# Two chained transformer blocks on one core: in the paired FFN products, high parts a piece ahead of low parts, two of four block sums on GpSimd, and later transposes

## The chip, the cores and the metric

The kernel runs on one core of a Trainium2 chip. The metric is the device time of one execution in microseconds. Five engines take part: TensorE (PE in the profile; its weight loads are PEld), VectorE (DVE), ScalarE (ACT), GpSimd (POOL) and SyncE (SP), which here only issues DMAs. Each engine works through its own instructions in order and waits for the others by semaphores.

## The reference

Two blocks work on 256 tokens of width 2048, in float32. The first holds three attention branches, the second a gated recurrence, a convolution and the FFN in which the change lies:

```python
x = x + jnp.einsum('bse,ed->bsd', mixed, w_out[l])
h2 = _rmsnorm(x, ffn_norm_w[l])
g, u = jnp.split(jnp.einsum('bsd,df->bsf', h2, w_gate_up[l]), 2, axis=-1)
x = x + jnp.einsum('bsf,fd->bsd', jax.nn.silu(g) * u, w_down[l])
```

`w_gate_up` is 2048 x 11264 and `w_down` 5632 x 2048. The weights, 406 MB in all, are read once from HBM.

## The kernel before, in words

**Matrix products.** TensorE works in a reduced 32-bit format. To keep float32 accuracy each operand is split into a high part and a low part: ScalarE copies a weight block `raw` to the high part `wh` (rounded), VectorE subtracts to get the low part `wl` (raw - wh). Three matmuls stand for one: high x high, low x high, high x low (lines 139, 140, 142 in a plain product). A block is 2 x 128 rows by 512 columns; the two token halves of 128 make a block's product twelve matmuls of 128 x 512.

**Pieces and their order.** All products are cut into pieces, worked on in one order. `drive` goes over the pieces: it calls `feed`, which has loads issued while fewer than `nraw` raw blocks are live and has pieces split into `wh` and `wl` until `la` pieces beyond the present one are done; then `prod` issues the piece's matmuls, and `done` frees its buffers and, after the last piece of a product, evacuates the sums from PSUM. The engines run this order asynchronously; it only sets what stands behind what in each engine's queue. A piece's `split` calls `hl` (line 382), which issues `wh` on ScalarE and at once `wl` on VectorE.

**Slots.** 43 SBUF slots of 4 KB per partition hold the raw blocks, `wh`, `wl`, activations and temporary sums. They are handed out first in, first out: whoever gets a slot waits for the last reader of what was in it.

**Paired products.** The FFN has eleven column blocks j of 512 columns. For j = 0 gate and up are plain products. For j = 1 to 10 they are made together by a `Pair`, which saves matmuls with Winograd's variant of Strassen's scheme on the first eight of sixteen row blocks. There are four groups. Each has four pieces (`QuadPart`): g (the raw gate block, products P1 and P2), u (the raw up block, P3), t (sums u0 - g0 and u1 - u0, P5 and P7) and v (sums u1 - t0 and g1 - v0, P6 and P4). A product P is three matmuls, so a group has 21. `formt` and `formv` are the tiles of the sums; `teng` names the engine of each of the four sums, "v" for VectorE in all four. After each group comes one plain block of the gate half (`PairChunk`, lines 201 to 204, 12 matmuls), and after the four groups the four blocks of the other half. So a pair has 4 x 21 + 8 x 12 = 180 matmuls.

At the end of the four groups ScalarE copies P1, P5, P6 and P7 to SBUF (`ps`) and GpSimd adds them in four sums. After the last block of the gate half, VectorE adds these to P2 and P4 (`sg`), and ScalarE applies SiLU. After the last block of the other half VectorE does the same for up and multiplies (`up` and `sg`, two of each). Then `finish` has the result transposed by TensorE, four transposes at a time, into PSUM bank 7 (`sp`), and split into `ah` (ScalarE) and `al` (VectorE) for the down product. This runs as a side lane, the generator `later`: `side` is called after each piece except g and t and takes each lane one step further; `yield n` lets n such calls pass.

**Thirds.** Columns 0 to 3, 4 to 7 and 8 to 10 make three thirds; each is followed by its part of the down product `w_down` (plain chunks, `ah` and `al` as stationary operands). `wide`, called at the first pair, gives the pairs seven of the eight PSUM banks for sums, five raw blocks and four pieces of lead.

Of the kernel before, what the change touches and what calls it, by code (L numbers as in the profile page):

```python
# [9 lines left out]
F32 = mybir.dt.float32  # L10
F32R = mybir.dt.float32r
# [5 lines left out]
P = 128  # L17
# [10 lines left out]
RAW = 4  # L28
LA = 3
# [37 lines left out]
class Slots:  # L67


    def __init__(self, pool, n):  # L70
        self.pool, self.free, self.of, self.peak, self.n = pool, deque(range(n)), {}, 0, n
# [43 lines left out]
class Chunk(Piece):  # L115
# [4 lines left out]
        self.job, self.ks, self.n = job, ks, job.n  # L120
        self.w = job.w[ks[0] * P:(ks[-1] + 1) * P, job.n0:job.n0 + job.n].rearrange("(k p) n -> p k n", p=P)

    def split(self, b):
        self.wh, self.wl = b.hl(self.raw, len(self.ks), self.n)
        b.drop(self.raw)

    def prod(self, b, outs=None, tiles=range(2)):
# [90 lines left out]
class QuadPart(Piece):  # L218
# [2 lines left out]
    def __init__(self, pair, q, raws, names, first, last):  # L221
        self.pair, self.q, self.raws, self.names, self.first, self.last = pair, q, raws, names, first, last

    def split(self, b):
        g, u = self.raws.get("g"), self.raws.get("u")
        if self.w is not None:
            self.raws[self.kind] = self.raw
        if self.kind == "g":
            self.wh, self.wl = b.hl(self.raw, 2, 512)
        elif self.kind == "u":  # L230
            self.wh, self.wl = b.hl(self.raw[:, 1:2], 1, 512)
        elif self.kind == "t":
            t = self.raws["t"] = b.slots.get([P, 2, 512], F32, "formt")
            b.tt(t[:, 0], u[:, 0], g[:, 0], ALU.subtract, b.teng[0])
            b.tt(t[:, 1], u[:, 1], u[:, 0], ALU.subtract, b.teng[1])
            self.wh, self.wl = b.hl(t, 2, 512)
        else:
            t, v = self.raws["t"], b.slots.get([P, 2, 512], F32, "formv")
            b.tt(v[:, 0], u[:, 1], t[:, 0], ALU.subtract, b.teng[2])
            b.tt(v[:, 1], g[:, 1], v[:, 0], ALU.subtract, b.teng[3])  # L240
            self.wh, self.wl = b.hl(v, 2, 512)
            b.drop(g)
            b.drop(u)
            b.slots.put(t, v)

    def prod(self, b):
        P_, q = self.pair.p, self.q
# [42 lines left out]
class Builder:  # L290
    def __init__(self, nc, tc, I, out, ctx):
        self.nc, self.tc, self.I, self.out = nc, tc, I, out
        pool = lambda name, bufs, **k: ctx.enter_context(tc.tile_pool(name=name, bufs=bufs, **k))
        self.pc = pool("const", 1)
        self.pw = pool("work", 2)
        self.pps = pool("ps", 1, space=bass.MemoryType.PSUM)
        self.abanks, self.sbanks, self.bof = deque(range(4)), deque(range(4, 8)), {}
        self.pd = pool("dram", 1, space=bass.MemoryType.DRAM)
        self.slots = Slots(pool("slots", 1), NSLOT)
        self.events = set()  # L300
        self.urgent, self.lanes = [], []
        self.debt = {"a": 0.0, "v": 0.0, "g": 0.0, "p": 0.0}
        self.jobs = []
        self.pre = {}
        self.teng = "vvvv"


    @staticmethod
# [70 lines left out]
        for t in ts:  # L379
            self.abanks.append(self.bof.pop(id(t))[1])  # L380

    def hl(self, src, nk, n):

        wh, wl = self.slots.get([P, nk, n], F32R, "wh"), self.slots.get([P, nk, n], F32R, "wl")
        self.nc.scalar.activation(wh, src, AF.Copy)  # L385
        self.nc.vector.tensor_tensor(wl, src, wh.bitcast(F32), op=ALU.subtract)  # L386
        return wh, wl

    def drop(self, raw):
        self.slots.put(raw)  # L390
# [82 lines left out]
    def split_first(self, k):  # L473

        p = self.all[0]
        if k == 0:
            p.wh, p.wl = self.slots.get([P, KG, 512], F32R, "wh"), self.slots.get([P, KG, 512], F32R, "wl")
        self.act(p.wh[:, k], p.raw[:, k])
        self.tt(p.wl[:, k], p.raw[:, k], p.wh[:, k].bitcast(F32), ALU.subtract)
        if k == KG - 1:  # L480
            self.drop(p.raw)
            self.ns = 1

    def feed(self, n):

        while True:
            while self.nd < len(self.loads) and self.live < self.nraw:
                self.load()
            if self.ns >= min(n, len(self.all)):
                break  # L490
            self.all[self.ns].split(self)
            self.ns += 1

    def drive(self):
        self.all = [p for j in self.jobs for p in j.pieces()]
        self.loads = [p for p in self.all if p.w is not None]
        self.nd = self.ns = self.live = 0
        self.nraw, self.la = RAW, LA
        self.feed(0)
        self.begin()  # L500
        for i, p in enumerate(self.all):
            if p.begin:
                p.begin()
            self.feed(i + 1 + min(self.la, 1 + i // RAMP))
            if type(p) is Chunk and p.job.evac is None:
                break
            for ev in p.needs:
                self.force(ev)
            p.prod(self)
            p.done(self)  # L510
            if p.side:
                self.side()

        for t in range(2):
            for c, p in enumerate(self.all[i:]):
                o = self.acc()
                p.prod(self, {t: o}, [t])
                self.last_evac(t, c, o)
                self.free(o)
            self.finish(t)  # L520
# [1289 lines left out]
    def ffn(self):  # L1810
# [19 lines left out]
        def finish(j, s):  # L1830
            h, l = sl.get([P, 4, 256], F32R, f"ah{j}"), sl.get([P, 4, 256], F32R, f"al{j}")
            aT[j] = (h, l)

            def later():
                for b in range(2):
                    yield 1
                    p = self.ps()
                    for jj in range(2):
                        for t in range(2):
                            self.tr(p[:, jj * 256 + t * P:jj * 256 + (t + 1) * P], s[:, t, (2 * b + jj) * P:(2 * b + jj + 1) * P])  # L1840
                    yield 1
                    fl = lambda a: a[:, 2 * b:2 * b + 2, :].rearrange("p a b -> p (a b)")
                    self.split(fl(h), fl(l), p)
                sl.put(s)
                self.done(f"aT{j}")
            self.add(later(), urgent=True)
            if j == 10:
                for v in h3 + list(self.sx.values()):
                    sl.put(*v)
# [44 lines left out]
        def wide():  # L1894

            self.abanks = deque(list(range(4, 7)) + list(self.abanks))
            self.sbanks = deque([7])
            self.nraw, self.la = 5, 4

        ak = lambda k: (aT[k // 4][0][:, k % 4, :], aT[k // 4][1][:, k % 4, :])  # L1900
        xs = lambda q, i: [v[:, i, q % 2, :] for v in self.sx[q // 2]]
# [91 lines left out]
```

## Time and profile before

| | us |
|---|---|
| three runs, median (lowest to highest) | 2350.32 (2348.36 to 2350.64) |
| the profiled execution | 2351.64 |
| its span, first to last instruction | 2349.4 |
| TensorE busy | 2254.9 (96%) |
| VectorE busy | 1541.1 (66%) |
| ScalarE busy | 1145.1 (49%) |
| GpSimd busy | 399.2 (17%) |
| mean granted TensorE clock | 0.984 |

Times in the views count from the start of the span. The FFN's first pair begins at 1562.5, and the pairs fill 1562.5 to 1724.3, 1813.5 to 2026.7 and 2114.9 to 2273.1; the down products lie between and behind them. A row of the lines view is a group of instructions of one line, engine and operation: its tile names (out <- in), count, busy time and mean in ns, and then the engine's idle time just before them and what ended it. A row of the timeline has start, duration, engine, line, tiles and count, and in brackets the idle time before it with its releaser. Matmuls overlap: one lasts 390 ns, but the next starts long before it ends, so the distance from start to start is its cost. A row of the windows view gives, for a stretch, its length, busy time of PE, PEld, DVE, ACT and POOL with counts, the granted clock and the DMA share.

### The profile page before, as it was taken

To read this page: it belongs to the slowest core of one execution; us is meant where nothing else is said; L and a number is where in the kernel's file an instruction comes from. 1 tells how busy PE (TensorE), PEld (TensorE's weight loads), DVE (VectorE), ACT (ScalarE), POOL (GpSimd) and SP (SyncE) were. 2 spreads that over 40 slices of the span, in tenths; PEclk is the share of its full clock that TensorE was granted. 3 is DMA by queue.
4 is the path that set the end of the run, shared out by engine and by line. 5 is a ranking of instruction groups with operands and counts; after the bars stand their busy time and mean duration, and the time that the engine had idled before them with its cause. 6 is when DMAs were issued, how large, how long until landed. Compare 5 with 4: busy or idle time off the path is not lost.

```text
span 2349.4 us, 27772 instructions
## 1 busy us (share of the span) xinstructions
PE 2254.9 (96%) x10396; PEld 1863.1 (79%) x10396; DVE 1541.1 (66%) x1774; ACT 1145.1 (49%) x1532; POOL 399.2 (17%) x284
## 2 busy tenths in 40 slices
PE   9999999999999999999999999998899888998898
PEld 7888888888888888888888888876678666786676
DVE  5775776456566554556867865657765777747774
ACT  6634545546545443445555544534453444534453
POOL 2020104004232010002733521101110111101111
PEclk9999999999999999999999999999999999999899
DMA  9655555464565566665455565645465444655472
GB/s 313 189 176 185 157 174 172 152 199 151 161 197 179 181 185 202 202 199 183 147 163 161 161 187 183 198 141 161 144 205 181 145 153 150 206 161 180 144 247 75
DMA packets 215046, 413.99 MB, mean 176 GB/s; under 512 B 13538, under 2 KB 20432, under 8 KB 214912
## 3 DMA queue, kind: packets, MB, share of 16 engines
q1 hardware_dynamic: 211968, 405.99, 54.5%
q0 software_dynamic: 2224, 5.13, 0.7%
q8 instruction: 81, 1.33, 0.2%
q10 hardware_dynamic: 720, 1.11, 0.1%
q14 instruction: 53, 0.43, 0.1%
HBM read 408.51 MB, written 3.67 MB: 175 GB/s over the span
## 4 chain that ended last, share of the span: by engine, by line
PE 66%; DVE 10%; ACT 5%; issue 4%; POOL 1%; ACTq 0%; DVEq 0%; POOLq 0%
PE acc L139 19%; PE acc L140 19%; PE acc L142 19%; DVE wl L386 5%; ACT wh L385 4%; PE sp L343 3%; DVE formv L318 2%; PE sp L363 2%; DVE formt L318 2%; POOL ps L318 1%; PE acc L201 1%; PE acc L202 1%; ACT ps L314 1%; PE acc L204 1%; DVE up L318 0%
## 5 line engine op out<-in xcount | busy, mean ns | idle before, releaser
L386 DVE TENSOR_TENSOR wl<-raw,wh 128x1024 fp32r<-128x1024 f32 (+2 forms) x763 | 956.5, 1292 | 318.2 <-ACT wh L385 274.6
L385 ACT ACTIVATE wh<-raw 128x1024 fp32r<-128x1024 f32 (+2 forms) x763 | 743.7, 1025 | 154.7 <-DVE wl L386 93.1
L139 PE MATMUL acc<-wh,xh 128*128 128x512 f32 (+2 forms) x864 | 339.8, 393 | 0.0
L140 PE MATMUL acc<-wh,xl 128*128 128x512 f32 (+2 forms) x864 | 336.2, 389 | 0.0
L142 PE MATMUL acc<-wl,xh 128*128 128x512 f32 (+2 forms) x864 | 230.5, 389 | 0.0
L139 PE MATMUL acc<-wh,h2h 128*128 128x512 f32 x512 | 202.2, 395 | 0.0
L140 PE MATMUL acc<-wh,h2l 128*128 128x512 f32 x512 | 199.4, 389 | 0.0
L142 PEld LDWEIGHTS acc<-wl,xh 128*128 128x128 f32 x864 | 162.8, 188 | 32.9
L140 PEld LDWEIGHTS acc<-wh,xl 128*128 128x128 f32 x864 | 162.7, 188 | 31.0
L139 PEld LDWEIGHTS acc<-wh,xh 128*128 128x128 f32 x864 | 162.7, 188 | 30.7
L318 POOL TENSOR_TENSOR ps<-ps 128x512 f32<-128x512 f32 x40 | 66.0, 1649 | 670.9 <-ACT ps L314 668.6
L139 PE MATMUL acc<-wh,ah 128*128 128x512 f32 x352 | 137.5, 391 | 0.0
L140 PE MATMUL acc<-wh,al 128*128 128x512 f32 x352 | 137.0, 389 | 0.0
L142 PE MATMUL acc<-wl,h2h 128*128 128x512 f32 x512 | 136.9, 389 | 0.0
L201 PE MATMUL acc<-wh,h3h 128*128 128x512 f32 x320 | 127.2, 397 | 0.0
L202 PE MATMUL acc<-wh,h3l 128*128 128x512 f32 x320 | 126.7, 396 | 0.0
L142 PEld LDWEIGHTS acc<-wl,h2h 128*128 128x128 f32 x512 | 96.1, 188 | 20.0
L385 ACT ACTIVATE wh<-formt 128x1024 fp32r<-128x1024 f32 x40 | 42.4, 1060 | 141.8 <-DVE formt L318 141.8
L140 PEld LDWEIGHTS acc<-wh,h2l 128*128 128x128 f32 x512 | 96.2, 188 | 18.9
L139 PEld LDWEIGHTS acc<-wh,h2h 128*128 128x128 f32 x512 | 96.2, 188 | 19.0
L385 ACT ACTIVATE wh<-formv 128x1024 fp32r<-128x1024 f32 x40 | 42.3, 1058 | 118.2 <-DVE formv L318 112.2
L142 PE MATMUL acc<-wl,ah 128*128 128x512 f32 x352 | 94.8, 389 | 0.0
(492 smaller groups left out, 3844.2 us busy)
## 6 DMA issues: line engine op xcount, KB each, us to landing
raw<-in_w_in_dram SPq DMA_DIRECT2D x328, 512.0 KB, 3.7
raw<-in_w_gate_up_dram SPq DMA_DIRECT2D x176, 512.0 KB, 4.1
raw<-in_w_down_dram SPq DMA_DIRECT2D x88, 512.0 KB, 4.0
raw<-in_w_out_dram SPq DMA_DIRECT2D x64, 512.0 KB, 3.8
raw<-in_w_branch_dram SPq DMA_DIRECT2D x48, 512.0 KB, 3.9
raw<-in_w_mem_kv_dram SPq DMA_DIRECT2D x31, 512.0 KB, 6.8
raw<-in_w_in_dram SPq DMA_DIRECT2D x8, 464.0 KB, 3.4
raw<-in_w_in_dram SPq DMA_DIRECT2D x8, 448.0 KB, 3.4
```

Of the source, the lines that this page charges most:

```text
L139: b.nc.tensor.matmul(outs[t], x, self.wh[:, kk], start=self.first and kk == 0, stop=False)
L140: b.nc.tensor.matmul(outs[t], y, self.wh[:, kk], start=False, stop=False)
L142: b.nc.tensor.matmul(outs[t], x, self.wl[:, kk], start=False, stop=self.last and kk == len(self.ks) - 1)
L201: b.nc.tensor.matmul(outs[t], x, self.wh[:, kk], start=self.first and kk == 0 and t == 1, stop=False)
L202: b.nc.tensor.matmul(outs[t], y, self.wh[:, kk], start=False, stop=False)
L204: b.nc.tensor.matmul(outs[t], x, self.wl[:, kk], start=False, stop=self.last and kk == len(self.ks) - 1)
L314: self.nc.scalar.activation(out, in_, func, **k)
L318: (self.nc.vector if eng == "v" else self.nc.gpsimd).tensor_tensor(out, a, b, op=op)
L343: self.nc.tensor.matmul(out, lhsT, rhs, start=start, stop=stop)
L363: self.nc.tensor.transpose(out, in_, self.ident if k == P else self.ident[:k, :k])
L385: self.nc.scalar.activation(wh, src, AF.Copy)
L386: self.nc.vector.tensor_tensor(wl, src, wh.bitcast(F32), op=ALU.subtract)
```

## The change

`split` becomes two steps, `hi` (the sums of t or v, then `wh`) and `lo` (`wl`). `feed` issues `hi` up to `ahead` pieces beyond the piece whose `lo` is due; `ahead` is 0 until `wide` sets it to 1. So from the first pair on, the high part of the next piece, with its sums, stands in the queues ahead of the low part of this one. `teng` becomes "ggvv": both sums of t go to GpSimd. And in `later` the first four transposes of a finished product are issued two side steps later (3 instead of 1). Nothing else is computed, and SyncE's order of loads is the same.

```diff
-    def split(self, b):
-        self.wh, self.wl = b.hl(self.raw, len(self.ks), self.n)
+    def hi(self, b):
+        self.src = self.raw
+        self.wh = b.hi(self.src)
+
+    def lo(self, b):
+        self.wl = b.lo(self.src, self.wh)
         b.drop(self.raw)
...
         elif self.kind == "t":
-            t = self.raws["t"] = b.slots.get([P, 2, 512], F32, "formt")
+            t = self.src = self.raws["t"] = b.slots.get([P, 2, 512], F32, "formt")
             b.tt(t[:, 0], u[:, 0], g[:, 0], ALU.subtract, b.teng[0])
             b.tt(t[:, 1], u[:, 1], u[:, 0], ALU.subtract, b.teng[1])
-            self.wh, self.wl = b.hl(t, 2, 512)
         else:
             t, v = self.raws["t"], b.slots.get([P, 2, 512], F32, "formv")
+            self.src = v
             b.tt(v[:, 0], u[:, 1], t[:, 0], ALU.subtract, b.teng[2])
             b.tt(v[:, 1], g[:, 1], v[:, 0], ALU.subtract, b.teng[3])
-            self.wh, self.wl = b.hl(v, 2, 512)
             b.drop(g)
             b.drop(u)
-            b.slots.put(t, v)
+        self.wh = b.hi(self.src)
+
+    def lo(self, b):
+        self.wl = b.lo(self.src, self.wh)
+        if self.kind in "tv":
+            b.slots.put(self.src)
...
-        self.teng = "vvvv"
+        self.teng = "ggvv"
...
-    def hl(self, src, nk, n):
-
-        wh, wl = self.slots.get([P, nk, n], F32R, "wh"), self.slots.get([P, nk, n], F32R, "wl")
+    def hi(self, src):
+
+        wh = self.slots.get(src.shape, F32R, "wh")
         self.nc.scalar.activation(wh, src, AF.Copy)
+        return wh
+
+    def lo(self, src, wh):
+        wl = self.slots.get(src.shape, F32R, "wl")
         self.nc.vector.tensor_tensor(wl, src, wh.bitcast(F32), op=ALU.subtract)
-        return wh, wl
+        return wl
...
-            self.all[self.ns].split(self)
+            while self.nh < min(self.ns + 1 + self.ahead, len(self.all)):
+                self.all[self.nh].hi(self)
+                self.nh += 1
+            self.all[self.ns].lo(self)
             self.ns += 1
...
-        self.nraw, self.la = RAW, LA
+        self.nraw, self.la, self.ahead = RAW, LA, 0
...
                 for b in range(2):
-                    yield 1
+                    yield 1 if b else 3
...
-            self.nraw, self.la = 5, 4
+            self.nraw, self.la, self.ahead = 5, 4, 1
```

Lines behind the change move by 8 to 16: a row of line 386 before is one of line 398 after, 385 is 393, 318 is 326 and 363 is 371.

What this does to VectorE's queue, in a group that follows the evacuation of the previous product. The rows begin with two raw blocks of 1024 columns (the last block and g) and one of 512 (u); `al` is the low part of the previous product's transposed result. Before:

```order
L386 TENSOR_TENSOR wl<-raw,wh 128x1024 x2
L386 TENSOR_TENSOR wl<-raw,wh 128x512
L318 TENSOR_TENSOR formt<-raw 128x512 x2
L386 TENSOR_TENSOR wl<-formt,wh 128x1024
L318 TENSOR_TENSOR al_15223<-sp,ah_15222 128x512
L318 TENSOR_TENSOR formv<-raw,formt 128x512
L318 TENSOR_TENSOR formv<-raw,formv 128x512
L386 TENSOR_TENSOR wl<-formv,wh 128x1024
L386 TENSOR_TENSOR wl<-raw,wh 128x1024 x2
L318 TENSOR_TENSOR al_15223<-sp,ah_15222 128x512
```

and after:

```order
L398 TENSOR_TENSOR wl<-raw,wh 128x1024 x2
L398 TENSOR_TENSOR wl<-raw,wh 128x512
L326 TENSOR_TENSOR formv<-raw,formt 128x512
L326 TENSOR_TENSOR formv<-raw,formv 128x512
L398 TENSOR_TENSOR wl<-formt,wh 128x1024
L398 TENSOR_TENSOR wl<-formv,wh 128x1024
L398 TENSOR_TENSOR wl<-raw,wh 128x1024 x2
L326 TENSOR_TENSOR al_15225<-sp,ah_15224 128x512
```

The two `formt` are gone from VectorE (on GpSimd eight of them stand in a row, then the four `ps` sums, then the next product's eight). The `formv` sums, which read `formt`, now stand ahead of `wl` of t, and `al` stands two raw blocks further back.

ScalarE's queue at the end of a product's gate half, where `sg<-sg` is the SiLU. Before:

```order
L314 ACTIVATE ps<-acc 128x512
L385 ACTIVATE wh<-raw 128x1024
L314 ACTIVATE sg<-sg,r_109 128x512 x2
L385 ACTIVATE wh<-raw 128x1024
L385 ACTIVATE wh<-raw 128x512
L385 ACTIVATE wh<-formt 128x1024
```

and after:

```order
L322 ACTIVATE ps<-acc 128x512
L393 ACTIVATE wh<-raw 128x1024
L322 ACTIVATE sg<-sg,r_109 128x512 x2
L393 ACTIVATE wh<-raw 128x512
L393 ACTIVATE wh<-formt 128x1024
L393 ACTIVATE wh<-formv 128x1024
```

The high part of the next product's first raw block stands ahead of the SiLU instead of behind it.

TensorE's queue at the first four transposes of the previous product's result (`sp<-ident,sg`); `sh` and `sl` are high and low parts of sums of activations, `h3h` and `h3l` those of the activations. Before, they stand behind piece u of the first group and ahead of piece t:

```order
L257 MATMUL acc<-wl,h3h_11861 128x512
L255 MATMUL acc<-wh,sh 128x512
L256 MATMUL acc<-wh,sl 128x512
L257 MATMUL acc<-wl,sh 128x512
L363 MATMUL sp<-ident,sg 128x128 x4
L255 MATMUL acc<-wh,sh 128x512
L256 MATMUL acc<-wh,sl 128x512
```

and after, behind the first plain block and ahead of the second group's g:

```order
L205 MATMUL acc<-wh,h3h_12227 128x512
L206 MATMUL acc<-wh,h3l_12228 128x512
L208 MATMUL acc<-wl,h3h_12227 128x512 x4
L371 MATMUL sp<-ident,sg 128x128 x4
L263 MATMUL acc<-wh,h3h_11861 128x512
L264 MATMUL acc<-wh,h3l_11862 128x512
```

The second four move from behind the first plain block to behind v of the second group:

```order
L263 MATMUL acc<-wh,h3h_11861 128x512
L264 MATMUL acc<-wh,h3l_11862 128x512
L265 MATMUL acc<-wl,h3h_11861 128x512
L371 MATMUL sp<-ident,sg 128x128 x4
L205 MATMUL acc<-wh,h3h_12227 128x512
L206 MATMUL acc<-wh,h3l_12228 128x512
```

More of the change, by code (lines that the diff above doesn't have):

```diff
@@ L222, in __init__, with hi @@
         self.pair, self.q, self.raws, self.names, self.first, self.last = pair, q, raws, names, first, last
-    def split(self, b):
+    def hi(self, b):
         g, u = self.raws.get("g"), self.raws.get("u")
@@ L228, in split @@
         if self.kind == "g":
-            self.wh, self.wl = b.hl(self.raw, 2, 512)
+            self.src = self.raw
         elif self.kind == "u":
-            self.wh, self.wl = b.hl(self.raw[:, 1:2], 1, 512)
+            self.src = self.raw[:, 1:2]
         elif self.kind == "t":
-            t = self.raws["t"] = b.slots.get([P, 2, 512], F32, "formt")
+            t = self.src = self.raws["t"] = b.slots.get([P, 2, 512], F32, "formt")
             b.tt(t[:, 0], u[:, 0], g[:, 0], ALU.subtract, b.teng[0])
             b.tt(t[:, 1], u[:, 1], u[:, 0], ALU.subtract, b.teng[1])
-            self.wh, self.wl = b.hl(t, 2, 512)
         else:
             t, v = self.raws["t"], b.slots.get([P, 2, 512], F32, "formv")
+            self.src = v
             b.tt(v[:, 0], u[:, 1], t[:, 0], ALU.subtract, b.teng[2])
             b.tt(v[:, 1], g[:, 1], v[:, 0], ALU.subtract, b.teng[3])
-            self.wh, self.wl = b.hl(v, 2, 512)
             b.drop(g)
             b.drop(u)
-            b.slots.put(t, v)
+        self.wh = b.hi(self.src)
[3 more added lines that the diff above has]
+            b.slots.put(self.src)
     def prod(self, b):
@@ L481, in split_first @@
             self.drop(p.raw)
-            self.ns = 1
+            self.ns = self.nh = 1
     def feed(self, n):
+        n = min(n, len(self.all))
         while True:
@@ L488, in feed @@
                 self.load()
-            if self.ns >= min(n, len(self.all)):
+            if self.ns >= n:
                 break
-            self.all[self.ns].split(self)
+            while self.nh < min(self.ns + 1 + self.ahead, len(self.all)):
+                self.all[self.nh].hi(self)
+                self.nh += 1
+            self.all[self.ns].lo(self)
             self.ns += 1
@@ L496, in drive @@
         self.loads = [p for p in self.all if p.w is not None]
-        self.nd = self.ns = self.live = 0
-        self.nraw, self.la = RAW, LA
+        self.nd = self.nh = self.ns = self.live = 0
+        self.nraw, self.la, self.ahead = RAW, LA, 0
         self.feed(0)
```

## The prediction

> **What bounds the kernel now.** I read the page first, for the shares over the whole span.
>
> ```profile
> span 2349.4 us, 27772 instructions
> PE 2254.9 (96%) x10396; PEld 1863.1 (79%) x10396; DVE 1541.1 (66%) x1774; ACT 1145.1 (49%) x1532; POOL 399.2 (17%) x284
> ```
>
> TensorE is busy 96% of the time, which seems to leave little. But a share is a mean over stages, so I cut the last stage, the FFN, at the first matmul of each paired product in the timeline of TensorE. The table by stages then has: products 1 to 3 together; product 4 alone and products 4 to 7; product 6 alone; the second down product; product 8 alone and 8 to 10; the rest.
>
> ```profile
> core 0: us, PE busy (x) PEld busy (x) DVE busy (x) ACT busy (x) POOL busy (x), PEclk, DMA share, GB/s
> 1562.50:1724.28 161.78, 137.28 (x565) 106.48 (x564) 124.90 (x141) 80.92 (x98) 19.78 (x12) 0.94 0.49 159
> 1813.50:1860.00 46.50, 42.74 (x181) 33.25 (x180) 35.94 (x40) 21.73 (x27) 6.61 (x4) 1.00 0.59 199
> 1813.50:2026.72 213.22, 182.41 (x745) 141.73 (x744) 164.49 (x184) 104.19 (x126) 26.39 (x16) 0.94 0.50 164
> 1915.14:1970.07 54.93, 46.30 (x190) 36.17 (x188) 42.32 (x48) 26.26 (x33) 6.59 (x4) 0.94 0.45 147
> 2026.72:2114.92 88.20, 88.20 (x394) 72.81 (x393) 48.34 (x49) 34.62 (x35) 0.00 (x0) 1.00 0.55 175
> 2114.92:2161.43 46.51, 42.76 (x182) 33.25 (x180) 35.93 (x40) 21.74 (x27) 6.60 (x4) 1.00 0.60 200
> 2114.92:2273.08 158.16, 138.11 (x557) 107.48 (x556) 122.17 (x136) 78.21 (x94) 20.87 (x14) 0.94 0.53 176
> 2273.08:2349.40 76.32, 66.60 (x297) 54.62 (x295) 41.75 (x52) 27.98 (x40) 6.27 (x6) 0.95 0.37 130
> ```
>
> The down product runs TensorE without a gap at clock 1.00. The paired products don't: 54.93 us for 180 matmuls and 8 transposes, clock 0.94. Products 4 and 8, which follow a down product, take 46.5 us each; the other eight take 161.78 + (213.22 - 46.50) + (158.16 - 46.51) = 440.15 us, 55.0 each. The timeline of TensorE in product 6 shows where the time goes and what a matmul costs:
>
> ```profile
> 1916.96 0.39 PE L257 MATMUL acc<-wl,sh 128*128 128x512 f32 x1
> 1922.38 0.30 PE L363 MATMUL sp<-ident,sg 128*128 128x128 f32 x1 [5.03 <-DVE sg L327]
> 1923.67 0.90 PE L363 MATMUL sp<-ident,sg 128*128 128x128 f32 x3 [1.00 <-DVE sg L327]
> ...
> 1925.66 0.63 PE L255 MATMUL acc<-wh,sh 128*128 128x512 f32 x1
> 1926.08 0.63 PE L256 MATMUL acc<-wh,sl 128*128 128x512 f32 x1
> ...
> 1929.49 0.39 PE L201 MATMUL acc<-wh,h3h 128*128 128x512 f32 x1
> ...
> 1932.21 0.60 PE L363 MATMUL sp<-ident,sg 128*128 128x128 f32 x4
> 1932.57 0.47 PE L255 MATMUL acc<-wh,h3h 128*128 128x512 f32 x1
> ```
>
> A block of twelve matmuls starts at 1929.49 and ends at 1932.21: 0.227 us each. Four transposes take 0.36. So a product's floor on TensorE is 180 x 0.227 + 0.72 = 41.5 us. It waits 6.03 us at the transposes of the previous product's `sg`, and then runs at 0.42 us per matmul (1925.66 to 1926.08) until about 1929.5, some twelve matmuls at 0.2 too much: 2.4 us. The rest, near 5 us, is in shorter waits. Yet TensorE is only the one that shows it. VectorE's groups in the same stretch say who sets the pace:
>
> ```profile
> L386 DVE TENSOR_TENSOR wl<-raw,wh 128x1024 fp32r<-128x1024 f32 (+1 forms) x16 | 17.7, 1145 | 2.5 <-ACT wh L385 2.5
> ...
> L318 DVE TENSOR_TENSOR formt<-raw 128x512 f32<-128x512 f32 x8 | 5.1, 684 | 0.0
> ...
> L386 DVE TENSOR_TENSOR wl<-formv,wh 128x1024 fp32r<-128x1024 f32 x4 | 4.9, 1226 | 4.7 <-ACT wh L385 4.7
> L386 DVE TENSOR_TENSOR wl<-formt,wh 128x1024 fp32r<-128x1024 f32 x4 | 4.9, 1224 | 4.7 <-ACT wh L385 4.7
> ...
> L385 ACT ACTIVATE wh<-formv 128x1024 fp32r<-128x1024 f32 x4 | 4.2, 1058 | 10.8 <-DVE formv L318 10.8
> ...
> L318 DVE TENSOR_TENSOR sg<-acc,ps 128x512 f32<-128x512 f32 x2 | 1.4, 684 | 0.6 <-POOL ps L318 0.6
> L318 DVE TENSOR_TENSOR al<-sp,ah 128x512 fp32r<-128x512 f32 x2 | 1.4, 684 | 0.0
> L314 ACT ACTIVATE ah<-sp 128x512 fp32r<-128x512 f32 x2 | 1.2, 578 | 0.0
> ```
>
> VectorE works 42.32 us and stands idle 12.5 (2.5 + 4.7 + 4.7 + 0.6), together the whole 54.9: a closed loop. It never waits for TensorE here. Of the idle time 9.4 us is one pattern, eight times 1.18 us: it makes a sum, ScalarE rounds the sum to its high part, and VectorE, next in line with the low part, stands until that is done.
>
> **The change, part by part.** All of it lies in the FFN. The up to 119 us above the floor, 440.15 - 8 x 41.5 = 108 and 2 x (46.5 - 40.8) = 11, are all that can be won.
>
> *High parts a piece ahead.* VectorE's order becomes: both `formv` sums, `wl` of t, `wl` of v. While ScalarE makes `wh` of v (1058 ns above), VectorE does `wl` of t (1.2 us: three in a row take 3.60, below), so at most 0.1 us of each 1.18 stays: minus 9.4 us a product, and minus most of the 2.5, because `wh` of the next product's first block now stands ahead of the two SiLU of `sg` on ScalarE. It adds no instruction. But each `wh` takes its slot a piece earlier, so the slot comes from a piece that TensorE finished more recently. That costs nothing while ScalarE and VectorE aren't five pieces ahead of TensorE, and in a loop that VectorE paces they aren't; in the down products, where they are, TensorE holds four finished pieces in hand.
>
> *Half of the sums to GpSimd.* VectorE loses eight sums, 5.1 us. GpSimd gets them: its 6.59 us in a product become some 20 of 45, so it isn't full. But the two engines disturb each other, and this is the dearest unknown. Three `wl` in a row without GpSimd, and three beside its sums in the earlier scan:
>
> ```profile
> 1955.29 3.60 DVE L386 TENSOR_TENSOR wl<-raw,wh 128x1024 fp32r<-128x1024 f32 x3
> ```
>
> ```profile
> 1331.03 6.23 DVE L386 TENSOR_TENSOR wl<-raw,wh 128x1024 fp32r<-128x1024 f32 x3
> ```
>
> ```profile
> 1332.04 2.09 POOL L318 TENSOR_TENSOR nkb<-nkb,nfb 128x512 f32<-128x512 f32 x1
> ```
>
> The three lose 2.63 us to about three GpSimd sums (two like the one shown; a third runs already at 1331.03): 0.88 us per sum, more than the 0.64 that VectorE itself needs (5.1 / 8). Bounds: 0 where the sums fall into VectorE's idle time, and 1.29, a whole sum undisturbed, where each stops VectorE for its length:
>
> ```profile
> L318 POOL TENSOR_TENSOR x<-x,gf 128x512 f32<-128x512 f32 x4 | 5.1, 1286 | 65.8 <-ACT sq L314 65.6
> ```
>
> I take 0.88, the dense case, since VectorE will have little idle time: plus 7.0 us. So this part alone gives 1.9 us back per product.
>
> *Transposes later.* The first four stand 24 matmuls (5.4 us) later, behind the first block of `PairChunk`, so the 6.03 us stall and the slow clock behind it go. In itself that wins nothing in a loop that VectorE closes; it lets TensorE use what VectorE delivers. The second four now stand behind v of the second group, and share bank 7 with the first four: they wait for `al`, which stands behind two more `wl` on VectorE. From the end of the last block VectorE has four instructions of evacuation (4 x 0.69), three `wl` (3.0), two `formv` with GpSimd beside them (1.4 + 1.8), four `wl` (4.8) and `al` (0.6): 14.4 us. TensorE is there after 54 matmuls and the first transposes, 54 x 0.227 + 0.36 = 12.6. So TensorE waits 1.8 us, but VectorE doesn't, and VectorE closes the loop: no term of its own.
>
> *A new wait.* The first two sums of the next product stand behind the four `ps` sums on GpSimd, which take 6.59 us and start only when the last group's P6 is copied. VectorE's first `formv` stands behind them, with the next product's `wl` and its evacuation queued behind it. Walking through the end of a product, I find: the four sums end some 7.6 us after the last group (0.6 for the copy and hops, 6.6, hops), the first new sum 1.3 later; VectorE has five `wl`, two `sg` and two more `wl` (6.0 + 1.4 + 1.9) to do until then, but starts on them about when the group ends on TensorE. That is 9.3 against some 9 to 11 us, as the copies come: a wait between 0 and 2. I book 1.0.
>
> *Last product.* In the last third only three products feed the down product, so its fifth block needs the transposes at once: transposes 0.36, `ah` 0.58, `al` 0.68, with hops about 1.7 us on TensorE, once. Between 0 and 2.5.
>
> **Sum.** VectorE per product: 42.3 - 5.1 + 7.0 = 44.2, plus 1.0 = 45.2 us, above TensorE's 41.5. Eight products: 440.15 - 8 x 45.2 = 78.6 us. Products 4 and 8 have no predecessor's `up` and `al` on VectorE and begin with four pieces in hand; I take 42.5 (between 40.8 and 46.5): 8.0. Minus 1.7: 84.9 us. The profiled execution took 2351.64 us, 1.3 above the median, within the run's spread: 2351.6 - 84.9 = **2266.7 us**.
>
> [...]
>
> **Rivals.**
> *Full blocking, GpSimd sets the pace.* Each sum costs VectorE 1.29: 8 x 1.29 = 10.3, so 47.5, and with GpSimd's sums themselves drawn out to 2.1 (row 1332.04) the first `formv` waits 1 us more: 49.5. Then 8 x 5.5 = 44, plus 4 for products 4 and 8, minus 2: 46 us, 2305. For it: the GpSimd sums are drawn out as well, from 1.29 to 2.09, so each engine waits for the other. Against it: over the dense stretch the price is 0.88. [...]
> *TensorE's floor.* If most GpSimd sums fall beside PSUM reads and idle time, VectorE needs 37.2 to 40 and TensorE 41.5 to 42.5. With 41.9: 105, plus 11: 2236. For it: nothing ties GpSimd's sums to VectorE's dense stretches. Against it: there is hardly anything else; `wl`, `formt` and `formv` are nine tenths of VectorE's work.
> *Slower.* Loads become the pace. If the raw blocks of a group are only released by the group before it, a group is a chain: landing 4.1 us, two sums 4.2, `formv` 1.4, `wh` 1.06, `wl` 1.2, v's matmuls 1.4: 13.4 us, against (46.5 - 4 x 2.72) / 4 = 8.9 in products 4 and 8. Four groups: 18 us more a product, less 8.4 in the eight that have the stall: 36 + 8 x 9.6 = 113 us, 2465. It decides if loads are issued less than a group ahead.
>
> ```profile
> raw<-in_w_gate_up_dram SPq DMA_DIRECT2D x176, 512.0 KB, 4.1
> ```
>
> ```profile
> DVE wl L386 <- ACT wh L385: 116.6, 113, 1.7
> ```
>
> Against it: VectorE's waits from 1562.5 to 2273, of which this is the largest, have no load among them.
>
> **How the numbers follow.** Paced by VectorE, 43.5 to 47 us a product, 2252 to 2281: 0.55. Floor: 0.22. GpSimd's pace: 0.17. Little or nothing won, because a wait that I don't see takes the place: 0.03. Slower: 0.03. A measurement of this kernel can tell 0.2% (4.7 us) from no change. The range, 2236 to 2305, runs from the floor to full blocking. Faster 0.94, same 0.03, slower 0.03.
>
> **What would show it.** Right: `wl` of `formt` and `formv` without the 4.7 us idle; `sp` of `sg` waits under 1 us in the first four, clock back to about 1.00 in the paired products; `wl` beside `formt` on GpSimd near 2.1 us; products of 45 us. Wrong: VectorE idle again, before `formv`, with GpSimd as the releaser (the first rival), or ScalarE waiting for loads.

## The result, and the profile after

| | us |
|---|---|
| before, four runs, median (lowest to highest) | 2349.76 (2348.36 to 2350.64) |
| after, four runs, median (lowest to highest) | 2278.99 (2277.85 to 2280.75) |
| ratio after / before, with its 95% interval | 0.9700 (0.9683 to 0.9717) |
| the profiled execution after | 2278.37 |

The change wins 70.8 us by the medians, 73.3 between the two profiled executions. The prediction had 84.9, with a time of 2266.7 and a range of 2236 to 2305. The first part of the page of after, the busy time of each engine and its share of the span:

```profile
span 2276.6 us, 27906 instructions
PE 2221.1 (98%) x10396; PEld 1848.0 (81%) x10396; DVE 1554.4 (68%) x1694; ACT 1145.2 (50%) x1532; POOL 540.2 (24%) x364
```

VectorE has 80 instructions fewer than before and yet 13 us more of busy time (1554.4 against 1541.1). That is the first sign of the price of GpSimd's help. The windows of after, cut as before at the first matmul of each product: products 1 to 3; product 4 alone and 4 to 7; products 5 and 6; product 8 alone and 8 to 10; the rest.

```profile
core 0: us, PE busy (x) PEld busy (x) DVE busy (x) ACT busy (x) POOL busy (x), PEclk, DMA share, GB/s
1561.51:1703.30 141.79, 128.59 (x566) 102.74 (x564) 129.19 (x119) 82.28 (x99) 56.60 (x34) 1.00 0.54 182
1791.33:1832.12 40.79, 40.79 (x181) 33.78 (x180) 37.03 (x33) 20.90 (x26) 18.45 (x11) 1.00 0.57 196
1791.33:1976.37 185.04, 169.82 (x745) 136.32 (x744) 169.82 (x154) 103.92 (x125) 76.48 (x44) 1.00 0.54 185
1832.12:1881.03 48.91, 43.29 (x189) 34.10 (x188) 44.83 (x41) 26.14 (x33) 20.59 (x12) 1.00 0.50 172
1881.03:1927.50 46.47, 42.62 (x190) 34.25 (x188) 42.29 (x41) 25.82 (x33) 20.35 (x12) 1.00 0.56 191
2064.36:2105.16 40.80, 40.80 (x182) 33.78 (x180) 37.04 (x33) 20.91 (x26) 18.46 (x11) 1.00 0.59 203
2064.36:2200.51 136.15, 126.64 (x557) 102.14 (x556) 125.31 (x114) 76.85 (x93) 57.41 (x34) 1.00 0.55 189
2200.51:2276.60 76.09, 66.40 (x297) 54.65 (x295) 42.03 (x53) 28.20 (x41) 6.27 (x6) 0.95 0.41 151
```

The granted clock in the paired products is 1.00 (before 0.94; the last column but two). Products 4 and 8 have TensorE busy from end to end: 40.8 us, its floor (180 matmuls at the prediction's 0.227 us). The other eight take 141.79 + (185.04 - 40.79) + (136.15 - 40.80) = 381.4 us, 47.7 each. So the eight won 58.8 us (predicted 78.6), products 4 and 8 won 11.4 (predicted 8.0), and the last stage 0.2 (predicted 1.7 lost). The other 2.4 us of the 72.8 between the spans lie ahead of the first pair and in the down products between the pairs.

In products 5 and 6 VectorE works 44.83 + 42.29 of 48.91 + 46.47 us: on average 43.6 busy and 4.1 idle. TensorE, with 43.0 busy, has come near. The chain of work that ended last, followed back from waiter to releaser, holds no matmul in product 6 of the kernel before and none in product 5 of after; in product 6 of after, 21.0 of its 46.5 us are matmuls and transposes. VectorE's groups in product 5 (count, busy us, mean ns; then the idle time before them and its releaser; this window cuts one more wait at its end, so `formv` shows two waits):

```profile
L398 DVE TENSOR_TENSOR wl<-raw,wh 128x1024 fp32r<-128x1024 f32 (+1 forms) x16 | 21.0, 1357 | 0.4 <-ACT wh L393 0.4
L326 DVE TENSOR_TENSOR formv<-raw,formt 128x512 f32<-128x512 f32 x5 | 6.7, 1335 | 2.4 <-POOL formt L326 2.4
L398 DVE TENSOR_TENSOR wl<-formt,wh 128x1024 fp32r<-128x1024 f32 x4 | 6.0, 1490 | 0.0
L398 DVE TENSOR_TENSOR wl<-formv,wh 128x1024 fp32r<-128x1024 f32 x4 | 4.9, 1221 | 0.1
...
L326 DVE TENSOR_TENSOR sg<-acc,ps 128x512 f32<-128x512 f32 x2 | 1.4, 688 | 2.0 <-POOL ps L326 2.0
```

The 4.7 us of idle time ahead of `wl` of t, and the 4.7 ahead of that of v, are gone, as predicted. Two other waits stand there now, both for GpSimd: 2.0 us ahead of `sg` and 1.2 ahead of the first `formv`. And the mean of `wl<-raw` has gone from 1145 to 1357 ns, that of `wl<-formt` from 1224 to 1490. The timeline around the end of product 5 shows both waits. VectorE:

```profile
1873.99 0.69 DVE L326 TENSOR_TENSOR sg<-acc,ps 128x512 f32<-128x512 f32 x1 [1.96 <-POOL ps L326]
...
1879.29 1.77 DVE L326 TENSOR_TENSOR formv<-raw,formt 128x512 f32<-128x512 f32 x1 [1.18 <-POOL formt L326]
1881.09 0.69 DVE L326 TENSOR_TENSOR formv<-raw,formv 128x512 f32<-128x512 f32 x1
```

GpSimd:

```profile
1870.81 6.75 POOL L326 TENSOR_TENSOR ps<-ps 128x512 f32<-128x512 f32 x4 [16.70 <-ACT ps L322]
1877.52 2.99 POOL L326 TENSOR_TENSOR formt<-raw 128x512 f32<-128x512 f32 x2
```

And ScalarE, then the last matmul of P6 on TensorE (those of P4 follow until 1867.20):

```profile
1866.26 2.00 ACT L393 ACTIVATE wh<-raw 128x1024 fp32r<-128x1024 f32 x2
1868.16 1.07 ACT L322 ACTIVATE ps<-acc 128x512 f32<-128x512 f32 x2
1869.11 1.06 ACT L393 ACTIVATE wh<-raw 128x1024 fp32r<-128x1024 f32 x1
1870.06 0.60 ACT L322 ACTIVATE ps<-acc 128x512 f32<-128x512 f32 x1
```

```profile
1866.53 0.39 PE L265 MATMUL acc<-wl,sh 128*128 128x512 f32 x1
```

The copy of P6 ends 3.7 us after TensorE is done with P6 (1870.66 against 1866.92). High parts stand ahead of the copies on ScalarE, which has no idle time in these rows. GpSimd's chain of four sums starts right behind it. VectorE waits inside that chain, and GpSimd itself had stood idle for 16.70 us just before. GpSimd has the time; it has it in the wrong place.

### The profile page after: what moved, and what is told of

The parts are those of the page before. It is cut to its first block, busy times and chain, and to the rows that moved or that the text cites. A ratio compares the mean times of both kernels' runs of the same rounds, so it can differ in the third digit from the quotient of the medians.

```text
span 2276.6 us, 27906 instructions
## 1 busy us (share of the span) xinstructions
PE 2221.1 (98%) x10396; PEld 1848.0 (81%) x10396; DVE 1554.4 (68%) x1694; ACT 1145.2 (50%) x1532; POOL 540.2 (24%) x364
## 4 chain that ended last, share of the span: by engine, by line
PE 73%; DVE 6%; ACT 3%; issue 3%; POOL 2%; ACTq 0%; POOLq 0%; DVEq 0%
PE acc L143 20%; PE acc L144 20%; PE acc L146 20%; DVE wl L398 3%; PE sp L351 3%; PE sp L371 2%; ACT wh L393 2%; DVE formv L326 2%; POOL ps L326 1%; PE acc L205 1%; PE acc L206 1%; PE acc L208 1%; PE acc L263 1%; PE acc L264 1%; PE acc L265 1%
## 5 line engine op out<-in xcount | busy, mean ns | idle before, releaser
L398 DVE TENSOR_TENSOR wl<-raw,wh 128x1024 fp32r<-128x1024 f32 (+2 forms) x763 | 989.7, 1338 | 298.4 <-ACT wh L393 253.0
L326 POOL TENSOR_TENSOR formt<-raw 128x512 f32<-128x512 f32 x80 | 141.8, 1793 | 328.8 <-DMA raw<-in_w_gate_up_dram 170.5
L393 ACT ACTIVATE wh<-formv 128x1024 fp32r<-128x1024 f32 x40 | 42.4, 1061 | 124.5 <-DVE formv L326 98.4
```

Of the source, the lines that this page charges most:

```text
L326: (self.nc.vector if eng == "v" else self.nc.gpsimd).tensor_tensor(out, a, b, op=op)
```

## The experiments

The theory, **V**: VectorE's own work and its waits make the product, so GpSimd's sums cost it about what they relieve it of, or more, and a stall of TensorE alone is worth nothing. Its rivals bear other letters in the expectations; the main ones are that the relief by GpSimd is what the change lives on (**G**) and that TensorE's stall and its clock make the time (**T**). The first six runs take the three parts of the change (A: high parts ahead; G: the t sums on GpSimd; T: late transposes) apart. Every ratio is against runs of the kernel before on the same chip, which had medians of 2349.36 to 2349.90.

**a1: without the GpSimd sums** (against the change).

```diff
-        self.teng = "ggvv"
+        self.teng = "vvvv"
```

> The changed kernel with all four block sums on VectorE again (high parts ahead and late transposes stay). Theory V (VectorE's work and its waits for ScalarE and GpSimd make the loop of a paired product; GpSimd's sums disturb VectorE as much as they relieve it, and the next product's sums queue behind the ps sums): VectorE works 42.3 us a product, the 2.4 us wait of formv for GpSimd goes, about 2.4 us of other waits stay, 44.7 instead of 47.7, so some 24 us faster than the changed kernel: 2255. Theory G (the sums on GpSimd are a gain, because VectorE has 5.1 us less to do): slower than the changed kernel by up to 8 x 5.1 = 41 us: 2320.

Measured: 2259.46 us, ratio 0.9615 (0.9601 to 0.9630). V held, though the time is 4.5 us above the one that it gave, and G fell: giving the sums back to VectorE makes the kernel 19.5 us faster. The windows of products 5 and 6 in a1:

```profile
1825.66:1869.94 44.28, 42.27 (x190) 34.42 (x188) 41.33 (x48) 25.65 (x32) 6.58 (x4) 1.00 0.57 190
1869.94:1915.42 45.48, 42.83 (x190) 34.27 (x188) 42.48 (x49) 26.29 (x32) 6.58 (x4) 1.00 0.57 192
```

VectorE does eight sums more per product than in the change and is busy 41.9 us instead of 43.6. Without its own sums (5.1) it would be 36.8, so GpSimd's eight cost it 6.8: 0.84 us each. Its idle time falls from 4.1 to 3.0 us: the 1.2 for `formt` is gone, the 2.0 for `ps` is not. Together 1.65 + 1.16 = 2.8 us a product in these two; the 19.5 us come to 2.4 in each of the eight.

**a2: without the high parts ahead.**

```diff
-            self.nraw, self.la, self.ahead = 5, 4, 1
+            self.nraw, self.la, self.ahead = 5, 4, 0
```

> The changed kernel with ahead = 0 (sums on GpSimd and late transposes stay). Theory V: wl of t no longer waits much, since GpSimd runs ahead of the order, but wl of v stands 1.2 us for wh of v again, and wh of the next product is behind the SiLU again: 4.7 to 7 us more a product, 52 to 55, about 2320 to 2340. Theory T (the late transposes are what wins): at most 10 us slower than the changed kernel, 2279 to 2289.

Measured: 2323.78 us, ratio 0.9890 (0.9875 to 0.9905). V held: nearly two thirds of the gain are gone. VectorE's groups in one product of a2 (1850.40 to 1902.13):

```profile
L398 DVE TENSOR_TENSOR wl<-formv,wh 128x1024 fp32r<-128x1024 f32 x4 | 8.1, 2017 | 4.7 <-ACT wh L393 4.7
L398 DVE TENSOR_TENSOR wl<-formt,wh 128x1024 fp32r<-128x1024 f32 x4 | 4.9, 1217 | 2.3 <-ACT wh L393 2.3
```

Here the same sums on GpSimd help: made early, they halve the wait for the high part of t (4.7 before). And the `wl` of v, which by this reading meets them, takes 2017 ns in the mean instead of 1226 before. Over the product VectorE is busy 41.50 us for 42.32 before, with eight sums of 0.64 fewer: here a sum on GpSimd costs it about 0.54 us, less than making it.

**a3: the first transposes early.**

```diff
-                    yield 1 if b else 3
+                    yield 1 if b else 1
```

> The changed kernel with the transposes at their old place (yield 1). Theory V: TensorE's stall for sg comes back, 4 to 5 us at the first four transposes, but it takes the place of other waits of TensorE in the same loop; what is left is the slow clock after it, 0 to 2.4 us a product: 2279 to 2298. Theory T: the whole stall and the slow clock, 8.4 us a product, come back: 2340 to 2346.

Measured: 2286.00 us, ratio 0.9725 (0.9709 to 0.9742). V held: the late transposes are worth 7 us in the change. TensorE's waits over products 5 and 6 of a3 (total us, times, longest) begin with

```profile
PE sp L371 <- DVE sg L335: 8.3, 4, 4.6
```

and the clock there is 0.93 and 0.96.

**a4: the late transposes alone** (against the kernel before; its `split` is in two steps with `ahead` 0, as in a6).

```diff
-                    yield 1
+                    yield 1 if b else 3
```

> The kernel before with only the transposes later. Theory V: VectorE's loop is untouched, 42.3 us of work and 12.5 of waits: no change within 5 us, 2345 to 2352. Theory T: 8 x 8.4 = 67 us faster, 2283.

Measured over ten runs: 2347.73 us, ratio 0.9990 (0.9980 to 0.9999). V held, T fell. The window of product 5, then the waits of TensorE over products 5 and 6:

```profile
1858.99:1915.58 56.59, 47.57 (x190) 35.86 (x189) 43.19 (x49) 26.93 (x33) 6.58 (x4) 0.94 0.46 149
```

```profile
PE acc L263 <- ACT wh L393: 8.6, 6, 2.9
PE acc L265 <- DVE wl L398: 3.7, 7, 0.5
PE sp L371 <- DVE al L326: 3.4, 2, 1.7
```

The 6 us stall for `sg`, the longest that TensorE showed before, isn't in the list. Yet only 2 us are won: TensorE now waits for weight blocks instead, and the clock stays at 0.94. The two-step `split` was not run by itself; a4 contains it.

**a5: the high parts ahead alone** (against the kernel before: `ahead` 1 from the first pair, `teng` and the transposes as before).

```diff
-            self.nraw, self.la = 5, 4
+            self.nraw, self.la, self.ahead = 5, 4, 1
```

> The kernel before with only the high parts a piece ahead (sums on VectorE, transposes at the old place). Theory V: VectorE's idle time falls from 12.5 to some 3 us a product, so nearly all of the gain is here: 2259 as without the GpSimd sums, plus 0 to 2.4 us a product for the slow clock after the stall at the transposes: 2259 to 2278, at or below the changed kernel. Theory P (the parts need each other: without the later transposes the stall of 6 us stays): 8 x 8.4 more, about 2325.

Measured: 2266.95 us, ratio 0.9648 (0.9634 to 0.9663). V held: this part alone is worth more than the whole change.

**a6: the GpSimd sums alone** (against the kernel before).

```diff
-        self.teng = "vvvv"
+        self.teng = "ggvv"
```

> The kernel before with only the sums of t on GpSimd (no high parts ahead, transposes at the old place). Theory V: as without the high parts ahead, 2324, plus 0 to 8 us for the slow clock after the stall: 2320 to 2332. Theory G (relief of VectorE by 5.1 us a product): 2350 minus 41 or more, 2309 or below.

Measured: 2334.56 us, ratio 0.9935 (0.9920 to 0.9950), 2.6 above the range that V gave, and far above what G gave. Still, 15 us are won where VectorE has waits to fill, as in a2.

The eight combinations, medians in us:

| | neither A nor G | G | A | A and G |
|---|---|---|---|---|
| transposes as before | 2350 | 2334.6 | 2267.0 | 2286.0 |
| transposes late | 2347.7 | 2323.8 | 2259.5 | 2279.0 |

G wins 15 to 24 us without A and loses 19 with it. The reading that fits a1 and a2: both feed on the same idle time of VectorE; once A has taken it, G only adds its price. T is worth 2 us alone, 7 to 11 beside A or G.

The next runs ask how a1, the best so far, or the change could lose their waits on GpSimd.

**a7: the t sums of each product's first group on VectorE** (against the change; the second sum likewise). This is to take away the wait at `formv` and a quarter of the disturbance.

```diff
-            b.tt(t[:, 0], u[:, 0], g[:, 0], ALU.subtract, b.teng[0])
+            b.tt(t[:, 0], u[:, 0], g[:, 0], ALU.subtract, b.teng[0] if self.q else "v")
```

> The changed kernel with the sums of the first group of each product on VectorE, the other three groups on GpSimd. Theory Q (half of the loss by GpSimd is the queue: the first sums stand behind the ps sums, and formv waits 2.4 us a product for them): the wait goes, 1.2 us of work comes to VectorE, and the disturbance of two sums goes with them: 1.5 to 2.5 us a product less than the changed kernel, 2259 to 2267. Theory S (only the number of sums on GpSimd counts): a quarter of the 19.5 us between the changed kernel and the one with its own sums: 2274.

Measured: 2269.18 us, ratio 0.9657 (0.9641 to 0.9673), between the two expectations. The waits for `formt` are gone from the list; half of the 19.5 us is won. Where the other half stays shows when the windows are cut at VectorE's own rhythm, from the second SiLU of one product to that of the next. Two such stretches of a7, from product 4 to 5 and from 5 to 6, then 5 to 6 of a1:

```profile
1821.27:1869.14 47.87, 43.12 (x189) 33.99 (x188) 44.87 (x42) 25.94 (x32) 17.79 (x11) 1.00 0.48 167
1869.14:1914.97 45.83, 42.83 (x185) 34.57 (x184) 42.83 (x42) 26.28 (x32) 17.43 (x11) 0.96 0.55 182
```

```profile
1861.87:1907.41 45.54, 42.89 (x190) 34.33 (x189) 42.53 (x48) 26.29 (x33) 6.59 (x5) 1.00 0.53 185
```

VectorE is idle 3.0 us in all three; the length follows its busy time. From 5 to 6 the six sums on GpSimd cost only 0.3 us more than in a1, where VectorE makes all of them; from 4 to 5 they cost 2.3. (The stretches that hold a down product lose 1.7 each.) So the price of a sum depends on what it meets, and 0.84 is a mean.

**a8: an early sum** (against a1: P7 + P1 as soon as t is copied, so that only one sum stands between P6's copy and the first `sg`, five in all).

```diff
+            if self.kind == "t":
+                p1, p7 = P_["P1s"], P_["P7s"]
+                b.tt(p7, p7, p1, ALU.add, "g")
...
+                b.tt(p7, p7, p6, ALU.add, "g")
                 b.tt(p6, p6, p1, ALU.add, "g")
-                b.tt(p7, p7, p6, ALU.add, "g")
```

> All block sums on VectorE, high parts ahead, late transposes, and GpSimd adds P1 to P7 as soon as both are copied, so that after the last copy, P6, one sum instead of two stands ahead of VectorE's evacuation (one GpSimd sum more in all). VectorE now waits 2.0 us a product there. Theory V: the wait falls to about 0.4: 1.6 us times 8 = 13 us less than 2259.5: 2247. Theory E (TensorE's floor and its waits at the second transposes set the time by now): no change, 2257 to 2261.

Measured: 2261.81 us, ratio 0.9626 (0.9611 to 0.9640): no gain, as E had it and against V. The wait went as hoped, over two products of a8 (its lines stand 3 further down than in the change):

```profile
DVE sg L329 <- POOL ps L329: 1.2, 2, 0.6
```

But VectorE's busy time in product 5 went from 41.33 to 43.05 us: the sums now fall beside its work (the two `formt` behind `sg`, beside which GpSimd's five sums now run on, take 3.47 us instead of 2.38).

**a9: the second four transposes later too** (against a1).

```diff
-                    yield 1 if b else 3
+                    yield 2 if b else 3
```

> All block sums on VectorE, high parts ahead, late transposes, and the second four transposes one step later still, where al is long done. TensorE now waits 1.6 to 2 us a product there. Theory V: TensorE's wait only reflects VectorE's loop, no change: 2256 to 2261. Theory E: 8 x 1.6 = 13 us less, 2246.

Measured: 2255.89 us, ratio 0.9601 (0.9587 to 0.9616), 3.6 below a1, at the edge of what V had, and far from E. TensorE's wait at these transposes (1.6 us a product in a1), which the prediction gave no term, is worth little.

**a11: two pieces of lead instead of four in the last group** (against a9), so that fewer high parts stand ahead of the copies on ScalarE.

```diff
-            self.feed(i + 1 + min(self.la, 1 + i // RAMP))
+            la = 2 if type(p) is QuadPart and p.last else self.la
+            self.feed(i + 1 + min(la, 1 + i // RAMP))
```

> Sums on VectorE, high parts ahead, both sets of transposes late (the fastest so far, 2255.9), and two instead of four pieces of lead while TensorE works on the last group of a product, so that the copies of P5, P7 and P6 stand behind three high parts fewer or so on ScalarE; VectorE's order stays. Theory K (VectorE waits 2.0 us for the ps sums because P6 is copied some 3 us late, behind high parts that nobody needs yet): the wait falls by 1 to 2 us a product, 2240 to 2248. Rival W (the wait is the length of two GpSimd sums, 3.4 us, and goes only with a shorter chain): no change, 2253 to 2259.

Measured: 2256.13 us, ratio 0.9601 (0.9587 to 0.9615). The wait for `ps` is gone from VectorE's list, as K had it; but the time stayed, as W had it. GpSimd's sums, in a9 and then in a11 (the windows of product 5 begin at 1826.29 and 1826.34), and the two `wl` ahead of `sg` on VectorE in a11:

```profile
1860.74 6.81 POOL L326 TENSOR_TENSOR ps<-ps 128x512 f32<-128x512 f32 x4 [38.28 <-ACT ps L322]
```

```profile
1858.83 8.64 POOL L326 TENSOR_TENSOR ps<-ps 128x512 f32<-128x512 f32 x4 [36.39 <-ACT ps L322]
```

```profile
1859.73 4.26 DVE L398 TENSOR_TENSOR wl<-raw,wh 128x1024 fp32r<-128x1024 f32 x2 [0.21 <-ACT wh L393]
```

With the copies first, GpSimd starts 1.9 us earlier, so the order on ScalarE did hold its sums back by that much. But now they meet the two `wl`, which take 4.26 us instead of 2.35, and the four sums take 8.64 instead of 6.81. VectorE comes to `sg` later, which is part of why it no longer waits there. Over products 5 and 6 it is busy 1.4 us a product more than in a9: the wait has become disturbance.

**a12: the price by itself** (against a9, with VectorE's work unchanged): GpSimd makes the two t sums besides, into a bfloat16 tile `extra` that nothing reads (its allocation is left out here).

```diff
+            b.nc.gpsimd.tensor_tensor(b.extra, u[:, 0], g[:, 0], op=ALU.subtract)
+            b.nc.gpsimd.tensor_tensor(b.extra, u[:, 1], u[:, 0], op=ALU.subtract)
```

> The same as the fastest so far (sums on VectorE, high parts ahead, both sets of transposes late), and GpSimd makes the two sums of t besides, into a tile that nobody reads (it is bfloat16). So VectorE is relieved of nothing and waits for none of it. Theory L (a GpSimd sum that reads SBUF stops VectorE's two-input work, 0.85 us each): VectorE's work rises from 42.0 to 48.8 a product, eight products get 5 to 7 us longer and products 4 and 8 up to 4: 2300 to 2315. Theory Q (the loss in the changed kernel is the queue, not the disturbance): 2256 to 2264.

Measured: 2324.85 us, ratio 0.9894 (0.9878 to 0.9911). L held in kind and Q fell, though the cost is 10 us above L's range: sums that no one uses or waits for cost 69 us. Products 5 and 6 of a9, then of a12:

```profile
1826.29:1870.12 43.83, 42.71 (x189) 34.34 (x188) 41.14 (x48) 25.64 (x32) 6.58 (x4) 1.00 0.56 192
1870.12:1915.25 45.13, 43.23 (x189) 34.18 (x188) 42.35 (x49) 26.30 (x32) 6.57 (x4) 1.00 0.57 195
```

```profile
1848.43:1900.47 52.04, 45.52 (x189) 34.71 (x188) 49.36 (x49) 25.50 (x32) 18.50 (x12) 0.97 0.47 162
1900.47:1954.25 53.78, 45.91 (x190) 34.85 (x188) 51.00 (x49) 26.14 (x33) 19.37 (x13) 0.97 0.48 162
```

The same VectorE instructions take (49.36 + 51.00 - 41.14 - 42.35) / 2 = 8.4 us more a product, 1.05 us for each of the eight sums, and the product 8.4 us longer; its idle time stays at 2.7. TensorE and ScalarE have the same instructions as in a9. Two `formv` of a12, one beside a GpSimd sum and one alone:

```profile
1901.79 1.77 DVE L329 TENSOR_TENSOR formv<-raw,formt 128x512 f32<-128x512 f32 x1
...
1916.63 0.68 DVE L329 TENSOR_TENSOR formv<-raw,formt 128x512 f32<-128x512 f32 x1
```

**a13: nothing on GpSimd in the products** (against a11: the four `ps` sums on VectorE too).

```diff
-                b.tt(p6, p6, p1, ALU.add, "g")
+                b.tt(p6, p6, p1, ALU.add, "v")
...
```

> The kernel with the copies first, and the four ps sums of each product on VectorE too, so that GpSimd has no part in the products. In that kernel VectorE works 43.3 us a product on average and waits about 1. Theory L (GpSimd's four sums cost VectorE about as much by disturbing it as VectorE would need for them): four sums of 0.64 come, 2.6 us, and the disturbance of the ps sums goes, 1.4 us that the copies first had brought and some 0.9 of before: no change within 5 us, 2251 to 2261. Theory R (GpSimd relieves VectorE of the ps sums at little cost): 8 x 2.6 = 21 us slower, 2277.

Measured: 2255.91 us, ratio 0.9598 (0.9585 to 0.9611). L held, R fell: with GpSimd idle in every product nothing is lost. Three kernels (a9, a11, a13) stand at 2256, 23 us below the change. The stretch from SiLU to SiLU, product 5 to 6, in a9, a11 and a13:

```profile
1862.13:1907.36 45.23, 43.33 (x190) 34.24 (x190) 42.44 (x48) 26.30 (x32) 6.58 (x5) 1.00 0.52 180
```

```profile
1864.69:1909.84 45.15, 43.29 (x190) 34.19 (x189) 43.81 (x49) 26.25 (x33) 8.39 (x5) 1.00 0.53 180
```

```profile
1865.52:1910.60 45.08, 43.25 (x189) 34.19 (x188) 43.37 (x53) 26.18 (x33) 0.00 (x0) 1.00 0.55 187
```

VectorE makes the four sums itself in a13 and is still busy 0.4 us less than in a11. But the length is the same in all three while its busy time goes from 42.4 to 43.8, and TensorE is busy 43.3. So VectorE's busy time alone no longer sets it. Whether they share a limit beyond that was not tried.

## Why the prediction was right or wrong

- **Who sets the pace: right, for the kernel before.** The argument was weaker than it looks: work and idle time add up to the whole stretch for any engine. What tells is that none of VectorE's waits in product 6 before is for TensorE, that a4 took TensorE's stall away and won 2 us, and that a12, which adds only GpSimd sums that nobody reads, lengthens VectorE's work and the product by the same 8.4. In the versions with high parts ahead TensorE is nearly level: a1 and a7 still follow VectorE's work, with 3.0 us idle in each, but a9, a11 and a13 don't.
- **High parts a piece ahead: right.** `wl` of t and v no longer waits (9.4 us a product before, 0.1 in product 5), and the 2.5 ahead of `wl` of the raw blocks fell to 0.4. Alone (a5) this wins 82 us. One premise didn't hold: that taking slots earlier costs nothing because ScalarE doesn't run far ahead. In the change ScalarE's `wh` does wait for TensorE's matmuls in the pairs (17.2 us in 5 waits, the longest 3.8); before, `wh` never waits for a matmul of a pair.
- **Half of the sums to GpSimd: right, price near.** The prediction took 0.88 us per sum for the disturbance; a1 gives 0.84, a12 1.05. That it came so near is partly luck: it was read from three sums in another stage, and a2 and a7 show that the price depends on where the sums fall. VectorE's busy time came to 43.6 for the predicted 44.2. The prediction's "alone gives 1.9 us back per product" reads like a gain, but its sum (42.3 - 5.1 + 7.0 = 44.2) has it as a loss of 1.9. Measured (a1) are 1.65 of busy time; with the wait that it brings (1.2) the part costs 2.8.
- **The waits: the step that was mis-sized.** The term "A new wait" has "I book 1.0", and nothing else of VectorE's idle time is left in the 45.2 us. Measured are 4.1: 1.2 before `formv` (the booked one, within its bounds of 0 to 2), 2.0 before `sg`, and 0.9 in small ones. The wait before `sg` was 0.6 us and was dropped with the 12.5 us of idle time; it grew instead. The order on ScalarE is at least part of the cause: with fewer high parts ahead of the copies (a11) GpSimd starts 1.9 us earlier and the wait vanishes, in part because VectorE comes later. The working priced the early `wh` on ScalarE for what VectorE gains, and not for what stands behind it there. Eight times 47.7 - 45.2 = 2.5 is the 20 us that the eight products fell short.
- **Transposes later: half right.** Alone they win 2 us (a4). But "in itself wins nothing" doesn't carry over to the whole: beside A they are worth 7 us. The slow clock behind the stall before was 0.50 (1925.66 to 1929.49). In the change without them (a3) TensorE's waits reach 4.6 us and the clock in products 5 and 6 is 0.93 and 0.96; how much of the 7 us is the clock was not taken apart. The 1.8 us wait at the second four came out at 1.9 in the mean (15.5 us in 8 waits, row at the end), and moving them (a9) wins 3.6, near the "no term" of the prediction.
- **Products 4 and 8: too careful by 3.4 us in all**; they run at TensorE's floor. **The last product's 1.7 us** wasn't seen: the last stage is as long as before.
- **The start of the sum and its total.** The sum starts from the profiled execution, 2351.64, which is not within the spread of the runs, as it says, but 1.0 above the highest. What was won beyond the booking outside the eight products hides part of their 20 us: in all the profiled execution came out 11.6 us short (73.3 for 84.9).
- **The signs to look for.** The idle ahead of `wl` gone, clock 1.00: both came. So did a sign that was to tell for the first rival, VectorE idle before `formv` with GpSimd as the releaser. Yet GpSimd doesn't set the pace: it stands idle for 16.70 us ahead of the `ps` sums. Products of 45 us did not come: 47.7.

The first rival's full blocking, 1.29 us of VectorE's time for each sum, was the author's assumption. At a single meeting the trace comes near it: after the first `formt` sum VectorE's `formv` starts at 1879.29; GpSimd's second ends at 1877.52 + 2.99 = 1880.51, and `formv` at 1881.06, 0.55 us later, a little under the 0.68 us that it takes alone (a12, row 1916.63). But no run shows 1.29 us a sum over a product: the mean is 0.84 (a1) to 1.05 (a12), and the time that the prediction drew from full blocking (2305) was too high by 26 us.

## What to carry to other kernels

In a closed loop, count an engine's work and its waits for others together: a stall on the engine that merely shows the loop can be removed without any gain, and a wait that is dropped from the sum must be followed to what will stand ahead of its releaser. Work moved to an idle engine may cost the busy one more than it relieves it of: here, with high parts ahead, a sum on GpSimd cost VectorE 0.84 us in the mean (a1), and doing it itself 0.64, while the sums on GpSimd won 15 us (a6) to 24 us (a2 against a4) where VectorE had idle time to give. Try each part of such a change alone: one part of this one wins more than all of it.

## What the runs showed of the hardware

- Sums on GpSimd whose result nobody reads slow the kernel by 69 us (a12 2324.85, a9 2255.89): of two `formv` in a12, which read two SBUF tiles, the one beside a GpSimd sum takes 1.77 us (row 1901.79), the one with GpSimd idle 0.68 (row 1916.63). With one input in PSUM no such difference shows: `sg<-acc,ps` takes 0.69 us beside the `ps` sums (after, row 1873.99), `up<-acc,ps` 0.68 with GpSimd idle (before, product 6). GpSimd's own sums are longer too: its `formt` sums take 1793 ns in the mean, as the page of after has it, against 1286 for the four `x<-x,gf` of that shape at the end of the kernel before.

```profile
L326 POOL TENSOR_TENSOR formt<-raw 128x512 f32<-128x512 f32 x80 | 141.8, 1793 | 328.8 <-DMA raw<-in_w_gate_up_dram 170.5
```

- Disturbance and waiting are exchanged for one another: a8 and a11 shortened VectorE's wait for GpSimd by 1.4 and 2.0 us a product, and its instructions became 1.7 and 1.4 us longer.
- In these runs the length of a wait alone doesn't decide TensorE's clock. TensorE's waits of up to 2.6 us (the first row below, from after's waits between 1562 and 2260) left the clock at 1.00 in its paired products; waits of up to 4.6 us (a3) go with 0.93 and 0.96. But nearly the same wait of 2.6 us, in after and then in a7, is followed by a clock of 1.00 in the one and of 0.66 over the next 5 us in the other. What decides was not tried.

```profile
PE sp L371 <- DVE al L326: 15.5, 8, 2.6
```

```profile
1898.40 0.66 PE L371 MATMUL sp<-ident,sg 128*128 128x128 f32 x4 [2.62 <-DVE al L326]
```

```profile
1899.00:1904.00 5.00, 5.00 (x24) 4.10 (x23) 4.71 (x7) 4.12 (x5) 0.76 (x1) 1.00 0.17 50
```

```profile
1894.29 0.66 PE L371 MATMUL sp<-ident,sg 128*128 128x128 f32 x4 [2.64 <-DVE al L326]
```

```profile
1895.00:1900.00 5.00, 5.00 (x16) 3.95 (x15) 4.71 (x7) 4.12 (x5) 0.87 (x1) 0.66 0.22 49
```
